# Two-layer decoder trunk: q and k halves of a pair run together, values a pair later, weight gaps behind first blocks, last gate pieces in two PSUM banks

## The chip, the cores and the metric

One Trainium2 chip, one core of it. The metric is device time in microseconds of one launch of the whole kernel; smaller is better. The time before is the median of three runs, and one further execution was profiled.

## The reference

Two pre-norm residual layers on a sequence of 256 tokens with width 1024, all in float32. Layer 0 mixes tokens with forgetting attention (a cumulative log gate is added to the causal logits), layer 1 with block attention, whose one block of 256 holds the whole sequence, so that it is causal attention with a T5 relative bias. Each layer is followed by a SwiGLU of width 2816 and a gated per-layer input.

```python
for i in range(DEPTH):                                  # DEPTH = 2
    u = _rmsnorm(h, attn_norm_g[i])
    proj = u @ w_in                                     # 1024 -> q, k, v (layer 0: and 16 forget logits)
    o = attention(q, k, v)                              # 16 heads of 64, causal, softmax in float32
    h = h + _merge_heads(o) @ w_o
    u = _rmsnorm(h, ffn_norm_g[i])
    gu = u @ ffn_w_in[i]                                # 1024 -> 2 x 2816
    h = h + (jax.nn.silu(gu[..., :D_FF]) * gu[..., D_FF:]) @ ffn_w_out[i]
    gate = jax.nn.sigmoid(_rmsnorm(h, ple_norm_g[i]) @ ple_w_gate[i])
    h = h + gate * (p[i] @ ple_w_up[i])
return _rmsnorm(h, final_norm_g)
```

## The kernel before, in words

**Numbers.** A float32 product is made of three passes in the faster type fp32r: each operand is split into a rounded part `hi` and a rest `lo`, and `mm3` issues hi*hi, hi*lo and lo*hi (lines 82, 83 and 84). Transposes (`tp`, `pp`), a part of the scores (`sp<-qkt`, line 409), of the values (`po<-tf,vf`, line 458) and a few small products (`pb`, `pr`) run in plain float32.

**Weights.** They come from DRAM in 216 halves of 128 x 1024 floats, in the order of use. `half` (lines 122 to 139) issues the load of one on SyncE's queue into `raw` (six buffers), ScalarE writes its rounded copy to `whi`, VectorE the rest to `wlo` (six buffers each, used as rings). Eight blocks of 128 x 128 lie in a half that is used as stationary operand. `APART = 16` sets where the first of them begins in its buffer, in elements of four bytes. A half that `blocks(entry)` loads with entry on has its first two blocks of `wlo` 8 elements further (`FURTHER`) and the other six 64 further (`LINE`); `whi` stays as it was.

**Attention.** First the values for all heads (`v`, four PSUM banks), then eight pairs of heads. For pair j, `project(j, 0)` makes q and `project(j, 1)` k: 8 blocks of 3 matmuls of 256 columns each, 24 per half, into one bank `pq`; behind the second VectorE and ScalarE scale and split them (`qkt`, `qkh`, `qkl`). `scores(j)` multiplies q and k of both heads on 64 rows of the array (`sp`; in layer 0 the gate is added by a further matmul), and VectorE and ScalarE make the softmax into `e`. `transposes(j)` turns the probabilities (`pp`, evacuated as `th`, `tl`, `tf`), `values(j)` multiplies them with the values (`po`). These steps are staggered, in an order written out by hand (lines 461 to 471):

```python
for j in range(NP):
    project(j, 0)
    if j >= 1:
        scores(j - 1)
    if j >= 2:
        transposes(j - 2)
    project(j, 1)
    if j >= 2:
        values(j - 2)
```

Behind the loop the remaining steps of pairs 5 to 7 alternate with halves of the output projection (`wo`).

**SwiGLU.** 22 blocks of 128 columns, `gu`: 24 matmuls for the gate and 24 for the up part. Blocks 0 and 1 run interleaved by k, with the transposes `tp` of the second half of `h` in front of k = 3. Between block 2's two halves stand the small fp32 products `pr` that spread the norm. From block 4 on, two blocks (96 matmuls of 256 columns) alternate with two steps of the down projection (`fo`, 512 columns). Of block 2 the second half, and of each even block from 4 on the first half, is loaded with entry on.

**End.** The gate of layer 1 ends in four pieces of 256 columns (two groups of rows t, two column pieces i): `part(t, i)` applies the sigmoid (`pgt`, line 601), multiplies and adds on VectorE (lines 602, 603), and squares and sums for the final norm on ScalarE (`sqf`, line 635). GpSimd makes the norm's factor (`colf`, lines 670, 671), then the rows are scaled (lines 672 to 676) and written out (line 653). Both pieces of t = 1 lie in one bank. PSUM has eight banks, all of one pool. Tiles wait for their buffers by semaphores; the engines otherwise run their queues in order.

Of the kernel before, what the change touches and what calls it, by code (L numbers as in the profile page):

```python
# [27 lines left out]
F32 = mybir.dt.float32  # L28
# [4 lines left out]
P = 128  # L33
# [24 lines left out]

ENTRY = 2
FURTHER = 8  # L60


@with_exitstack
def trunk(ctx: ExitStack, tc: tile.TileContext, x, xt, pt, w, wf, cst, pick, gains, gf, bf, rel, hot, rvm, out):
# [50 lines left out]
    def half(at=0, entry=0):  # L115


        i = state["next"]
        state["next"] += 1
        raw = work.tile([P, HW], F32, tag="raw", bufs=RAW, name=f"raw{i}")  # L120
        hi = work.tile([P, HW + LINE], F32R, tag="whi", bufs=6, name=f"whi{i}")[:, at:at + HW]
        lt = work.tile([P, HW + 2 * LINE], F32R, tag="wlo", bufs=6, name=f"wlo{i}")
        lo = lt[:, at:at + HW]
        if entry:
            nc.sync.dma_start(raw, w[i])
            nc.scalar.activation(hi, raw, AF.Copy)  # L126
            ats = [(at + FURTHER, 0, entry), (at + LINE, entry, HW)]
            for a, c0, c1 in ats:
                nc.vector.tensor_tensor(lt[:, a + c0:a + c1], raw[:, c0:c1], f32(hi[:, c0:c1]), op=ALU.subtract)  # L129
            return hi, [lt[:, a + k * P:a + (k + 1) * P] for a, c0, c1 in ats for k in range(c0 // P, c1 // P)]  # L130
        parts = 2 if i < 2 else 1
        for q in range(parts):
            c = slice(q * HW // parts, (q + 1) * HW // parts)
            if i == 0 and q == 1:
                nc.sync.dma_start(hx[:, 1], xt[:, 1])
            nc.sync.dma_start(raw[:, c], w[i][:, c])
            nc.scalar.activation(hi[:, c], raw[:, c], AF.Copy)  # L137
            nc.vector.tensor_tensor(lo[:, c], raw[:, c], f32(hi[:, c]), op=ALU.subtract)  # L138
        return hi, lo

    def blocks(entry=False):

        hi, lo = half(APART, ENTRY * P if entry else 0)
        hi = [hi[:, k * P:(k + 1) * P] for k in range(KT)]
        return hi, lo if entry else [lo[:, k * P:(k + 1) * P] for k in range(KT)]

# [91 lines left out]
    for t in (f32(vhi), f32(vlo), vf):  # L238
        nc.gpsimd.memset(t[:, :, DH:2 * DH], 0.0)

    fh, fl = (one.tile([P, KT, 4, 32], F32R, name=n) for n in ("fh", "fl"))
    for t in (fh, fl):
        nc.gpsimd.memset(f32(t)[:, :, :, H:], 0.0)

    def split(hi, lo, src):
# [25 lines left out]
    def fox_bias(nm):  # L271


        split(fh[:, :, :, 0:H], fl[:, :, :, 0:H], wf32.unsqueeze(2).to_broadcast([P, KT, 4, H]))
        pf = bank("pf")
# [59 lines left out]
    def attention(layer, nm, mid, early, nf):  # L335
# [49 lines left out]
        def project(j, a):  # L385
            hi, lo = blocks()
            if a == 0:
# [107 lines left out]
    def ffn(layer, nm, filler, np_):  # L495
# [3 lines left out]
        def up(fs):  # L499
# [96 lines left out]
    def ple(layer, nm, ut, nx):  # L596

        def gate(bk, t, c0, c1):
            at = slice(c0, c1)
            sg = work.tile([P, HC], F32, tag="t2k", bufs=3, name=f"pgt{layer}_{t}_{c0}")[:, 0:c1 - c0]  # L600
            nc.scalar.activation(sg, bk[:, c0 % HC:(c1 - 1) % HC + 1], AF.Sigmoid, scale=nm.col[:, t:t + 1])
            nc.vector.tensor_tensor(sg, sg, ut[:, t, at], op=ALU.mult)
            nc.vector.tensor_tensor(h[:, t, at], h[:, t, at], sg, op=ALU.add)

        bks = [[bank(f"pg{layer}_{hf}_{t}") for t in range(2)] for hf in range(2)]
# [26 lines left out]
        def square(t, i, c0, c1):  # L632

            sq = work.tile([P, HC], F32, tag="t2k", bufs=3, name=f"sqf{t}_{i}")
            nc.scalar.activation(sq[:, 0:c1 - c0], h[:, t, c0:c1], AF.Square, scale=D ** -0.5,
                                 accum_out=ss[:, t, i:i + 1])
# [7 lines left out]
        def part(t, i):  # L644
            c0 = HC + i * S
            gate(bks[1][t], t, c0, c0 + S)
            square(t, 1 + i, c0, c0 + S)
            if i == 0:
                nc.vector.tensor_tensor(ms[:, t, 1:2], ms[:, t, 0:1], ss[:, t, 1:2], op=ALU.add)
                nc.vector.tensor_tensor(ys[:, t, HC:HC + S], h[:, t, HC:HC + S], gb[:, HC:HC + S], op=ALU.mult)  # L650

        def rows(t, c0, c1, queue):
            queue.dma_start(out[t * P:(t + 1) * P, c0:c1], ys[:, t, c0:c1])

        for t in range(2):
            if t == 0:
                for c in range(4):
                    pair_unit(bks[1], c, wts[c], nm.k, (t,))
                part(t, 0)
            else:  # L660
                for i in range(2):
                    for k in range(KT):
                        c0 = (k % 2) * HC + i * S
                        tokens(bks[1][t][:, i * S:(i + 1) * S], nm.k(k), t, [w[:, c0:c0 + S] for w in wts[k // 2]],
                               k == 0, k == KT - 1)
                    if i == 0:
                        part(t, 0)
            part(t, 1)
            r = col[:, t:t + 1]
            nc.gpsimd.tensor_tensor(r, ss[:, t, 2:3], ms[:, t, 1:2], op=ALU.add)  # L670
            nc.gpsimd.tensor_tensor(r, r, nhalf[:, 0:1], op=ALU.pow)
            nc.scalar.activation(ys[:, t, 0:HC], ys[:, t, 0:HC], AF.Copy, scale=r)
            rows(t, 0, HC, nc.scalar)
            nc.vector.scalar_tensor_tensor(ys[:, t, HC + S:D], h[:, t, HC + S:D], r, gb[:, HC + S:D],
                                           op0=ALU.mult, op1=ALU.mult)
            nc.vector.tensor_scalar(ys[:, t, HC:HC + S], ys[:, t, HC:HC + S], r, None, op0=ALU.mult)
            rows(t, HC, D, nc.sync)

    for layer in range(2):
# [8 lines left out]
        nm = Norm(3) if layer == 0 else None  # L688
        ple(layer, np_, got[0], nm)


# [93 lines left out]
```

## Time and profile before

| | us |
|---|---|
| median of 3 runs | 674.04 (673.87 to 674.23) |
| the profiled execution | 674.86 |
| its span, first to last instruction | 673.0 |
| TensorE busy in the span | 661.4 |
| VectorE busy | 453.2 |
| ScalarE busy | 385.8 |

The profile is of one execution. In a row of the timeline stand the start and the duration in us, the engine (PE is TensorE's matmul, PEld its weight load, DVE VectorE, ACT ScalarE, POOL GpSimd, SP SyncE), the line, the operation, and output<-inputs with shape and count; in brackets, idle time of the engine before it and what ended it. Matmuls are pipelined: each lasts longer than the distance to the next, so that the distance between starts is what one costs. A row of the stages gives a window, its length, then each engine's busy time and count, the granted clock, the share of the DMA engines and GB/s. A row of the waits gives who waited for whom: total us, times, longest. The granted clock over the span was 0.997.

### The profile page before, as it was taken

Reading aid. Unit: us, or ns where it says so; the run is one execution under the profiler, and the core shown is the slowest. Engines: PE = TensorE matmul, PEld = TensorE weight load, DVE = VectorE, ACT = ScalarE, POOL = GpSimd, SP = SyncE. Lnnn points to the kernel's source line nnn. Section 1 sums busy time; section 2 is a strip of 40 time slices with the busy share of each in tenths; the row PEclk is TensorE's granted clock in tenths of the full one; section 3 lists DMA queues with packets and bytes.
Section 4 is the critical chain, followed back from the end, with each engine's and each line's share of the span. In section 5 each row is a group of like instructions: output and inputs, shape, how many; then the busy total and the mean of one; then the engine's idle time right before and its main releaser. Section 6 shows DMA issues by size and latency. Waiting matters only on the chain.

```text
span 673.0 us, 11820 instructions
## 1 busy us (share of the span) xinstructions
PE 661.4 (98%) x4620; PEld 607.0 (90%) x4620; DVE 453.2 (67%) x804; ACT 385.8 (57%) x697; POOL 10.0 (1%) x26
## 2 busy tenths in 40 slices
PE   8999999999999999999999999999999999999994
PEld 6889998999999999998889999889999999999884
DVE  5688775676666666666676888765766666666673
ACT  6876675564444444547666766655544444454663
POOL 2000000000000000000000000000000000000000
PEclk9999999999999999999999999999999999999998
DMA  8976334456555556555585533353755555565401
GB/s 277 384 279 237 126 127 129 153 170 207 193 196 195 199 188 208 193 197 174 185 286 199 172 127 126 107 175 107 241 195 193 197 197 188 188 212 195 173 1 62
DMA packets 37063, 123.78 MB, mean 184 GB/s; under 512 B 4288, under 2 KB 7056, under 8 KB 37008
## 3 DMA queue, kind: packets, MB, share of 16 engines
q1 hardware_dynamic: 36128, 121.35, 53.3%
q10 hardware_dynamic: 848, 1.68, 0.7%
q8 instruction: 36, 0.59, 0.3%
q14 instruction: 19, 0.16, 0.1%
q0 software_dynamic: 32, 0.01, 0.0%
HBM read 121.94 MB, written 4.22 MB: 187 GB/s over the span
## 4 chain that ended last, share of the span: by engine, by line
PE 92%; DMA 3%; ACT 2%; DVE 1%; issue 1%; SPq 0%; POOLq 0%; DVEq 0%; POOL 0%; ACTq 0%
PE gu L83 12%; PE gu L82 12%; PE gu L84 12%; PE fo L83 6%; PE fo L82 6%; PE fo L84 6%; PE pq L82 4%; PE pq L84 4%; PE pq L83 4%; DMA raw<-w 2%; PE wo L82 2%; PE wo L84 2%; PE wo L83 2%; PE pg L82 2%; PE pg L84 2%; PE pg L83 2%
## 5 line engine op out<-in xcount | busy, mean ns | idle before, releaser
L138 DVE TENSOR_TENSOR wlo<-raw,whi 128x1024 fp32r<-128x1024 f32 (+1 forms) x198 | 239.7, 1214 | 141.1 <-ACT whi L137 140.9
L137 ACT ACTIVATE whi<-raw 128x1024 fp32r<-128x1024 f32 (+1 forms) x198 | 207.2, 1050 | 159.3 <-PE gu L83 46.7
L82 PE MATMUL gu<-g,whi 128*128 128x256 f32 x704 | 195.5, 278 | 0.0
L84 PE MATMUL gu<-g,wlo 128*128 128x256 f32 x704 | 195.1, 277 | 0.0
L83 PE MATMUL gu<-g,whi 128*128 128x256 f32 x704 | 195.1, 277 | 0.0
L82 PEld LDWEIGHTS gu<-g,whi 128*128 128x128 f32 x704 | 132.6, 188 | 0.8
L83 PEld LDWEIGHTS gu<-g,whi 128*128 128x128 f32 x704 | 132.3, 188 | 0.7
L84 PEld LDWEIGHTS gu<-g,wlo 128*128 128x128 f32 x704 | 132.2, 188 | 0.0
L82 PE MATMUL pq<-g,whi 128*128 128x256 f32 x256 | 73.9, 289 | 0.0
L84 PE MATMUL pq<-g,wlo 128*128 128x256 f32 x256 | 71.8, 280 | 0.0
L83 PE MATMUL pq<-g,whi 128*128 128x256 f32 x256 | 71.7, 280 | 0.0
L82 PE MATMUL fo<-whi,fh 128*128 128x512 f32 x176 | 68.9, 391 | 0.0
L83 PE MATMUL fo<-wlo,fh 128*128 128x512 f32 x176 | 68.7, 390 | 0.0
L84 PE MATMUL fo<-whi,fl 128*128 128x512 f32 x176 | 68.5, 389 | 0.0
L82 PEld LDWEIGHTS pq<-g,whi 128*128 128x128 f32 x256 | 48.1, 188 | 1.0 <-ACT vhi L373 0.6
L84 PEld LDWEIGHTS pq<-g,wlo 128*128 128x128 f32 x256 | 48.7, 190 | 0.0
L83 PEld LDWEIGHTS pq<-g,whi 128*128 128x128 f32 x256 | 48.4, 189 | 0.0
L246 ACT ACTIVATE fh<-sg 128x256 fp32r<-128x256 f32 x44 | 18.2, 418 | 48.5 <-DVE sg L533 48.5
L129 DVE TENSOR_TENSOR wlo<-raw,whi 128x256 fp32r<-128x256 f32 (+1 forms) x40 | 26.0, 688 | 22.8 <-ACT whi L126 22.8
L84 PEld LDWEIGHTS fo<-whi,fl 128*128 128x128 f32 x176 | 33.1, 188 | 7.1
L82 PEld LDWEIGHTS fo<-whi,fh 128*128 128x128 f32 x176 | 33.1, 188 | 6.3
L83 PEld LDWEIGHTS fo<-wlo,fh 128*128 128x128 f32 x176 | 33.1, 188 | 6.0
(146 smaller groups left out, 967.1 us busy)
## 6 DMA issues: line engine op xcount, KB each, us to landing
raw<-w SPq DMA_DIRECT2D x214, 512.0 KB, 3.3
d<-d SPq DMA_DIRECT2D x4, 768.0 KB, 7.8
bias<-d SPq DMA_DIRECT2D x4, 512.0 KB, 5.2
raw<-w SPq DMA_DIRECT2D x4, 256.0 KB, 5.2
h<-x ACTq DMA_DIRECT2D x2, 512.0 KB, 5.3
hx<-xt SPq DMA_DIRECT2D x3, 256.0 KB, 5.1
p<-pt SPq DMA_DIRECT2D x2, 256.0 KB, 3.5
end<-gf SPq DMA_DIRECT2D x1, 512.0 KB, 4.4
```

The costliest lines, as they stand in the source:

```text
L82: mm(o, ah, bh, start=start, stop=False, skip_group_check=True)
L83: mm(o, ah, bl, start=False, stop=False, skip_group_check=True)
L84: mm(o, al, bh, start=False, stop=stop, skip_group_check=True)
L129: nc.vector.tensor_tensor(lt[:, a + c0:a + c1], raw[:, c0:c1], f32(hi[:, c0:c1]), op=ALU.subtract)
L137: nc.scalar.activation(hi[:, c], raw[:, c], AF.Copy)
L138: nc.vector.tensor_tensor(lo[:, c], raw[:, c], f32(hi[:, c]), op=ALU.subtract)
L246: nc.scalar.activation(hi, src, AF.Copy)
```

## The change

1. **Order in attention.** A pair's two projections stand together; then values three pairs back, scores one pair back, transposes two pairs back. Behind the loop the order is written anew.
2. **Gaps.** A new loader `gapped` reads halves that lie in DRAM with 56 zero columns behind their first block (1080 columns; every row of the weight array in DRAM is now that long, and other halves read the first 1024). In `whi` and `wlo` alike the block used first begins 8 elements further than before and the other seven 64 further. It is used for the first half of pairs 2 to 7, for one half of SwiGLU block 0 (there with block 3, the first behind the transposes, moved to the front), and for the second half of block 2, which had entry on before.
3. **Buffers.** `raw` is 1088 columns wide, `whi` 1152; `fh` and `fl`, the split weights of the forget gate, lie in one place of the `whi` and `wlo` rings instead of tiles of their own.
4. **End.** The second column piece of t = 1 has a bank of its own (`pgl`). The first rows' scaling is put behind the last gate and the last square on ScalarE, as two pieces; their output is one DMA on SyncE's queue. The final norm's weights are multiplied in ahead for the last column piece too. The last four weight halves begin at element 48 (`AHEAD`) instead of 0.

```diff
-ENTRY = 2
 FURTHER = 8
+ENTRY = (0, 1)
+GAP = LINE - FURTHER
+WW = HW + GAP
+AHEAD = 48
...
+    def gapped(first=0):
+        i = state["next"]
+        state["next"] += 1
+        raw = work.tile([P, HW + LINE], F32, tag="raw", bufs=RAW, name=f"raw{i}")
+        at = slice(APART + FURTHER, APART + FURTHER + WW)
+        ht, lt = (work.tile([P, HW + 2 * LINE], F32R, tag=n, bufs=6, name=f"{n}{i}")[:, at] for n in ("whi", "wlo"))
+        nc.sync.dma_start(raw[:, 0:WW], w[i])
+        nc.scalar.activation(ht, raw[:, 0:WW], AF.Copy)
+        nc.vector.tensor_tensor(lt, raw[:, 0:WW], f32(ht), op=ALU.subtract)
+        cs = [bool(n) * GAP + n * P for n in (_entered(first).index(k) for k in range(KT))]
+        return [[t[:, c:c + P] for c in cs] for t in (ht, lt)]
...
         def project(j, a):
-            hi, lo = blocks()
+            hi, lo = gapped() if j > 1 and a == 0 else blocks()
...
         for j in range(NP):
             project(j, 0)
+            project(j, 1)
+            if j >= 3:
+                values(j - 3)
             if j >= 1:
                 scores(j - 1)
             if j >= 2:
                 transposes(j - 2)
-            project(j, 1)
-            if j >= 2:
-                values(j - 2)
...
+        wo(0, 0)
+        values(NP - 3)
+        scores(NP - 1)
+        wo(1, 0)
         transposes(NP - 2)
-        wo(0, 0)
-        scores(NP - 1)
+        wo(0, 1)
         values(NP - 2)
-        wo(1, 0)
-        wo(0, 1)
         transposes(NP - 1)
         wo(1, 1)
         wo(0, 2)
...
-                wts = {f: (blocks(), blocks()) for f in fs}
+                wts = {f: (blocks() if f else gapped(3), blocks()) for f in fs}
...
-                wt = blocks(a == 1 if fs[0] == 2 else a == 0 and fs[0] % 2 == 0)
+                if fs[0] == 2 and a:
+                    wt = gapped()
+                else:
+                    wt = blocks(ENTRY if fs[0] % 2 == 0 and a == 0 and fs[0] > 2 else ())
...
-        wts = [half() for _ in range(4)]
+        wts = [half(AHEAD) for _ in range(4)]
...
+        for c in range(4):
+            pair_unit(bks[1], c, wts[c], nm.k, (0,))
+        for i in range(2):
+            part(0, i, bks[1][0])
+        lb = (bks[1][1], bank("pgl"))
+        for i in range(2):
+            for k in range(KT):
+                c0 = (k % 2) * HC + i * S
+                tokens(lb[i][:, i * S:(i + 1) * S], nm.k(k), 1, [w[:, c0:c0 + S] for w in wts[k // 2]],
+                       k == 0, k == KT - 1)
+            last = part(1, i, lb[i])
+
+        for ins, c in zip(last, (slice(0, HC), slice(HC, D))):
+            with tc.issue_after(ins.ins):
+                nc.scalar.activation(ys[:, 0, c], ys[:, 0, c], AF.Copy, scale=col[:, 0:1])
+        rows(0, 0, D, nc.sync)
+        nc.scalar.activation(ys[:, 1, 0:HC], ys[:, 1, 0:HC], AF.Copy, scale=col[:, 1:2])
+        rows(1, 0, HC, nc.scalar)
+        nc.vector.tensor_scalar(ys[:, 1, HC:D], ys[:, 1, HC:D], col[:, 1:2], None, op0=ALU.mult)
+        rows(1, HC, D, nc.sync)
```

More of the change, by code (lines that the diff above doesn't have):

```diff
@@ L119, in half @@
         state["next"] += 1
[L120 to L123, printed above, removed]
+        raw = work.tile([P, HW + LINE], F32, tag="raw", bufs=RAW, name=f"raw{i}")
+        ht, lt = (work.tile([P, HW + 2 * LINE], F32R, tag=n, bufs=6, name=f"{n}{i}") for n in ("whi", "wlo"))
+        hi, lo = ht[:, at:at + HW], lt[:, at:at + HW]
         if entry:
-            nc.sync.dma_start(raw, w[i])
-            nc.scalar.activation(hi, raw, AF.Copy)
+            nc.sync.dma_start(raw[:, 0:HW], w[i][:, 0:HW])
+            nc.scalar.activation(hi, raw[:, 0:HW], AF.Copy)
             ats = [(at + FURTHER, 0, entry), (at + LINE, entry, HW)]
@@ L139, in half, with blocks @@
         return hi, lo
[L141 to L145, printed above, removed]
+    def blocks(entry=()):
+        hi, lo = half(APART, len(entry) * P)
+        return [[t[k] if isinstance(t, list) else t[:, k * P:(k + 1) * P] for k in range(KT)] for t in (hi, lo)]
+    def gapped(first=0):
+        i = state["next"]
+        state["next"] += 1
+        raw = work.tile([P, HW + LINE], F32, tag="raw", bufs=RAW, name=f"raw{i}")
+        at = slice(APART + FURTHER, APART + FURTHER + WW)
[5 more added lines that the diff above has]
+        return [[t[:, c:c + P] for c in cs] for t in (ht, lt)]
     class Norm:
@@ L271, in fox_bias @@
     def fox_bias(nm):
+        fh, fl = (work.tile([P, HW + 2 * LINE], F32R, tag=t, bufs=6, name=n)[:, 0:HW].rearrange(
+            "p (k r c) -> p k r c", k=KT, r=4) for n, t in (("fh", "whi"), ("fl", "wlo")))
+        for t in (fh, fl):
+            nc.gpsimd.memset(f32(t)[:, :, :, H:], 0.0)
         split(fh[:, :, :, 0:H], fl[:, :, :, 0:H], wf32.unsqueeze(2).to_broadcast([P, KT, 4, H]))
@@ L652, in rows @@
         def rows(t, c0, c1, queue):
             queue.dma_start(out[t * P:(t + 1) * P, c0:c1], ys[:, t, c0:c1])
[L655 to L677, printed above, removed]
@@ L689, in trunk, with _entered, _gapped @@
         ple(layer, np_, got[0], nm)
+def _entered(first):
+    return [first] + [k for k in range(KT) if k != first]
+def _gapped(a, first=0):
+    t = a.reshape(P, KT, P)[:, _entered(first)].reshape(P, HW)
+    return np.concatenate([t[:, :P], np.zeros((P, GAP), t.dtype), t[:, P:]], axis=1)
 def _rows(a):
@@ L739 @@
         seq += _rows(wi[:, 2 * D:3 * D])
[L740 removed]
+        seq += [_gapped(a) if n > 3 and n % 2 == 0 else a for n, a in enumerate(_cols(wi[:, :D], wi[:, D:2 * D]))]
         seq += [_wide(wo, 2 * c, hf) for hf, c in ((0, 0), (1, 0), (0, 1), (1, 1), (0, 2), (1, 2), (0, 3), (1, 3))]
         a = _cols(fin[i][:, :DFF], fin[i][:, DFF:])
+        a[0], a[5] = _gapped(a[0], 3), _gapped(a[5])
         o = _rows(fout[i])
```

27 lines of the change are left out of this document (14 added, 13 removed).

## The prediction

> **What bounds it now.** I read the page's first part, then the chain of waits, then TensorE's timeline, looking for the spacing of the matmuls' starts.
>
> ```profile
> span 673.0 us, 11820 instructions
> PE 661.4 (98%) x4620; PEld 607.0 (90%) x4620; DVE 453.2 (67%) x804; ACT 385.8 (57%) x697; POOL 10.0 (1%) x26
> PE 92%; DMA 3%; ACT 2%; DVE 1%; issue 1%; SPq 0%; POOLq 0%; DVEq 0%; POOL 0%; ACTq 0%
> ```
>
> TensorE has work queued nearly all the time and is 92% of the chain that ended last. So a change pays only if it shortens TensorE's own stream, removes one of its few stalls, or shortens the tail behind it. The stream does not run at one speed:
>
> ```profile
> 37.24 0.28 PE L84 MATMUL pq<-g,wlo 128*128 128x256 f32 x1
> 39.96 0.28 PE L84 MATMUL pq<-g,wlo 128*128 128x256 f32 x1
> 69.81 0.28 PE L83 MATMUL pq<-g,whi 128*128 128x256 f32 x1
> 72.40 0.28 PE L84 MATMUL pq<-g,wlo 128*128 128x256 f32 x1
> 145.23 0.28 PE L82 MATMUL gu<-g,whi 128*128 128x256 f32 x1
> 148.05 0.28 PE L82 MATMUL gu<-g,whi 128*128 128x256 f32 x1
> 159.10 0.28 PE L82 MATMUL gu<-g,whi 128*128 128x256 f32 x1
> 161.82 0.28 PE L82 MATMUL gu<-g,whi 128*128 128x256 f32 x1
> ```
>
> These are first and last rows of four unbroken stretches of the same shape. Pair 0's projections: 24 steps in 2.72 us, 113.3 ns each. A later pair: 22 steps in 2.59 us, 117.7 ns. SwiGLU block 3: 24 steps in 2.82 us, 117.5 ns. Block 4: 24 in 2.72 us, 113.3 ns. I call these the quick and the slow pitch, 4.3 ns apart. In the timeline a stretch keeps its pitch until something breaks the stream. Slow are: pair 1's second half and pairs 2 to 7 of both layers, and blocks 0 to 3 of both layers. All blocks from 4 on are quick, and those are the ones whose even member enters from `fo` with two blocks of `wlo` shifted by 8 elements.
>
> **Pitch in attention.** Pairs 0 and 1 now run as one stretch of 96 matmuls, so pair 1's second half (24) stays quick without any gap. Pairs 2 to 7 (6 x 48 = 288 matmuls) each enter behind an fp32 transpose or the scores, with block 0 of both `whi` and `wlo` 8 elements further. If that tips them to the quick pitch, a layer gains 312 x 4.3 = 1.34 us, and the six fp32r matmuls of `po` behind pairs 3 to 7 inherit it: 30 x 4.3 = 0.13. Tipping itself costs something:
>
> ```profile
> 156.35 0.28 PE L82 MATMUL gu<-g,whi 128*128 128x256 f32 x1
> 142.31 0.36 PE L82 MATMUL gu<-g,whi 128*128 128x256 f32 x1
> ```
>
> Block 4's first 24 take 159.10 - 156.35 = 2.75 us, 0.03 more than quick; six entries, 0.18. Net 1.3 us a layer, 2.6 in both. Against it: the half that starts at 142.31, behind the fp32 matmuls of `pr`, carries the same old shift of `wlo` and leads into the slow stretch at 145.23. So a shift of 8 is no guarantee behind fp32; the new form differs by shifting the `whi` block too.
>
> The Trainium skill ("TensorE: Matmul & The Clock Gate", Part 2, "What happens when you issue a matmul") gives TensorE two independent read ports, one for the moving operand and one for the weights; and "SBUF — State Buffer" (Specifications) 16-byte lines, on which a start 32 bytes further is as well aligned as before. By these the place of a block changes nothing. The two pitches of one shape above say that something besides shape counts, but not that this shift controls it; so it is a rival below.
>
> **Pitch in the SwiGLU.** Blocks 0 and 1 behind the transposes `tp` (k = 3 to 7, 60 matmuls), block 2's first half (24), then behind `pr` block 2's second half and block 3 (72): 156 x 4.3 = 0.67 us, less two entries of 0.03, so 0.6 a layer, 1.2 in both.
>
> **Regrouping.** Per pair the order was half, scores, transposes, half, values; it becomes half, half, values, scores, transposes.
>
> ```profile
> 67.81 0.28 PE L84 MATMUL pq<-g,wlo 128*128 128x256 f32 x1
> 68.02 0.49 PE L409 MATMUL sp<-qkt 64*128 64x128 f32 x4
> 68.26 0.37 PE L412 MATMUL sp<-qkh 64*128 64x256 f32 x2
> 68.46 0.29 PE L412 MATMUL sp<-qkl,qkh 64*128 64x256 f32 x2
> 68.98 0.87 PE L443 MATMUL pp<-ident,e 128*128 128x128 f32 x6
> 69.61 0.36 PE L82 MATMUL pq<-g,whi 128*128 128x256 f32 x1
> 72.52 0.28 PE L82 MATMUL po<-th,vhi 128*128 128x256 f32 x1
> 73.23 0.61 PE L458 MATMUL po<-tf,vf 128*128 128x128 f32 x4
> 73.59 0.36 PE L82 MATMUL pq<-g,whi 128*128 128x256 f32 x1
> ```
>
> Going from 128 rows to the scores' 64 the last projection takes 68.02 - 67.81 = 0.21 us instead of 0.12: 0.09 us. That switch is not removed: scores still come eight times a layer, now mostly behind `po`. Entering `po` costs nothing (72.40 to 72.52 is one slow pitch). Of two returns from fp32 to the projections a pair, one goes. A return takes 0.20 us for its first projection (69.61 to 69.81), 0.08 over the pitch, but just ahead of it the fp32 starts are packed closer (four in 0.36 us from 73.23 to 73.59, against six in 0.63 from 68.98 to 69.61), so it is worth between 0 and 0.08 a pair, and I take the low end: 0.05 us a layer for all regrouping. The trace has no step from fp32 on 128 rows to fp32 on 64; its bounds are no cost (the 10 of both layers' loops then gain 0.9 us more) and twice 0.09 (0.9 us less). I take 0.09, the nearest row.
>
> A stall does go:
>
> ```profile
> 42.89 0.49 PE L409 MATMUL sp<-qkt 64*128 64x128 f32 x4
> 44.41 0.39 PE L412 MATMUL sp<-qkl,qkh 64*128 64x256 f32 x2 [0.69 <-DVE qkl L247]
> 45.02 0.39 PE L82 MATMUL pq<-g,whi 128*128 128x256 f32 x1
> PEld po L458 <- ACT tf L448: 0.2, 1, 0.2
> ```
>
> The first scores of layer 0 took 45.02 - 42.89 = 2.13 us against 0.96 (68.02 to 68.98), waiting for VectorE's `qkl`. Now 24 more projections (2.72 us) stand ahead of them, over twice the excess, so 1.2 us goes. The 0.2 us wait of layer 1's values for `tf` goes too, because they stand a pair further back. Together 1.4.
>
> What is late next? At a pair's end ScalarE and VectorE now meet `qkt`, a weight half, `qkh`/`qkl`, the output, two softmaxes and the transposes' evacuation in a row.
>
> ```profile
> L138 DVE TENSOR_TENSOR wlo<-raw,whi 128x1024 fp32r<-128x1024 f32 (+1 forms) x198 | 239.7, 1214 | 141.1 <-ACT whi L137 140.9
> 56.44:99.96 43.52, 43.52 (x389) 41.88 (x388) 34.81 (x107) 29.65 (x82) 0.00 (x0) 1.00 0.40 134
> 72.35 0.42 ACT L448 ACTIVATE tf<-pp 128x128 f32<-128x128 f32 x2
> ```
>
> In this stage VectorE is busy 34.81 of 43.52 us, 80%; the pair becomes some 3% shorter, so about 82%. Transposes to values were 72.52 - 69.61 = 2.91 us, and `tf` came at 72.77, 0.25 us after values began but before their fp32 part. In the loop the distance becomes a whole pair of halves, 48 x 0.1133 = 5.4 us, and the values lie a step later as well: cover of over 2 us. Only behind the loop (`values(5)` one `wo` half behind `transposes(5)`, `values(6)` likewise) is it as short as before with the longer queue ahead: 0.1 us a layer lost, bounds 0 and 0.5. The gapped halves are 1080 columns instead of 1024, 5% more ScalarE, VectorE and DMA work for 8 of 54 halves a layer; DMA is busy 0.40 here and these engines are ahead of TensorE by several halves, so nothing; without that cover 5% of VectorE's 1.214 us for each of 16 halves, 1 us in all. `fh` and `fl` take one of the ring's six places early in layer 0; hidden as the ring is filled ahead, and one fill late, 1.2 us, if not.
>
> **The last pieces.**
>
> ```profile
> 658.06 0.28 PE L82 MATMUL pg<-whi,g 128*128 128x256 f32 x1
> 660.82 0.28 PE L84 MATMUL pg<-whi,g 128*128 128x256 f32 x1
> 662.50 0.39 PE L82 MATMUL pg<-whi,g 128*128 128x256 f32 x1 [1.40 <-ACT pgt L601]
> 665.36 0.28 PE L84 MATMUL pg<-whi,g 128*128 128x256 f32 x1
> 658.26 0.48 ACT L601 ACTIVATE pgt<-pg,col 128x256 f32<-128x256 f32 x1 [1.93 <-PE pg L84]
> 660.16 0.46 ACT L601 ACTIVATE pgt<-pg,col 128x256 f32<-128x256 f32 x1
> 661.99 0.46 ACT L601 ACTIVATE pgt<-pg,col 128x256 f32<-128x256 f32 x1
> 663.73 0.42 DVE L602 TENSOR_TENSOR pgt<-pgt,ut 128x256 f32<-128x256 f32 x1
> 665.67 0.47 ACT L601 ACTIVATE pgt<-pg,col 128x256 f32<-128x256 f32 x1 [0.52 <-PE pg L84]
> 668.54 0.72 ACT L672 ACTIVATE end<-end,colf 128x512 f32<-128x512 f32 x1 [0.94 <-POOL colf L671]
> 669.29 0.38 ACTq L653 DMA_DIRECT2D out<-end  x1
> ```
>
> The last 24 matmuls waited until 662.50 because they write the bank that the gate still reads. In a bank of their own they follow at once: the last starts at about 660.94 + 23 x 0.12 = 663.7, and its gate could start 0.31 later (665.36 to 665.67), at 664.0. But ScalarE is in order: gate, square, gate. The spacing of gates where nothing else held them is 660.16 - 658.26 = 1.90, so from 661.99 the last gate is free at 663.9. VectorE's multiply, now at 663.73 behind the first rows' scaling, moves up since that scaling is moved off VectorE, behind the last gate and the last square on ScalarE. So the last gate starts at 664.0, not 665.67: 1.7 us. From there to the last issue of a DMA (669.29) the chain is the same 3.6 us; the two moved scalings (0.72 each by the row at 668.54) fit into ScalarE's waits for `h` and for `colf`. The first rows' whole 512 KB now leave about 1 us before the last ones instead of 5 us; sharing the queues costs 0 to 0.4 us, and I take 0.1. Net 1.6. The shift AHEAD of 48 can speed these 48 matmuls, but ScalarE then holds the chain, so nothing.
>
> **Sum.** 2.6 + 1.2 + 0.1 + 1.4 - 0.2 + 1.6 = 6.7 us. The profiled execution took 674.86 us (span 673.0 and 1.9 around it), 0.82 above the median of 674.04. So 674.86 - 6.7 = 668.2 on that footing, 667.3 as a median.
>
> **Rivals.** (1) The gaps do not tip the stream behind fp32 work, as the half behind `pr` suggests. Then only pair 1's half remains of the pitch, 2 x 0.1, and 2.6 + 1.2 - 0.2 = 3.6 us is missing: 670.9. This is also the case that the change doesn't do what it says. Partly tipped, attention alone: 668.5; chance 0.15 for partly, 0.2 for not at all. For it: no entry behind fp32 with a shift is quick in this trace. Against: pair 0 (quick at 37.24) enters behind the fp32 matmuls of `pb`, so fp32 ahead does not forbid it. (2) Slower: bunched evacuations become a wait. Place: `values(j-3)` and the scores' banks wait for ScalarE and VectorE at every pair. VectorE's 20% idle must then not be usable in the new order. It decides when the wait exceeds 6.7 / 16 = 0.42 us a pair over 16 pairs; at 0.6 us it gives 677. The 1.07 us by which `qkl` was late once shows that such waits exist; the 2 us of cover speak against. Chance 0.04. (3) Rival 1 with about half of such a wait, which cancels: within 0.2%, chance 0.04.
>
> **Numbers.** My forecast has 0.57; 0.2% is 1.35 us, about what a measurement of this kernel can tell from no change. Faster: 0.57 + 0.15 + 0.2 = 0.92; same 0.04; slower 0.04. The range reaches down by the free switch (0.9) and the other bounds to 665.8, and up to include rival 1 at 671.0.
>
> **What would show it.** After: projections of pairs 2 to 7 at 113 ns, blocks 2 and 3 likewise; no wait of `sp` for `qkl`; no wait of `pg` for `pgt`; last gate 1.9 us behind the one before. Wrong if those stretches stay at 117.7, or TensorE shows waits at `po` or `sp`.

## The result and the profile after

| | us |
|---|---|
| before, median of 4 runs beside the changed kernel | 674.13 (673.87 to 674.28) |
| after, median of 4 runs | 669.68 (669.48 to 669.80) |
| ratio, 95% interval | 0.9933 (0.9917 to 0.9949) |
| profiled execution, before and after | 674.86 and 669.8 |

The change makes the kernel 4.45 us faster by the medians and 5.0 us by the spans of the two profiles; forecast were 667.3 and a range of 665.8 to 671.0. One later profiled execution, of a repeat of the changed kernel, was disturbed as a whole (2345.92 us) and no stage of it is used.

The page after has these lines on the bound:

```profile
span 668.0 us, 11833 instructions
PE 656.7 (98%) x4620; PEld 603.0 (90%) x4620; DVE 455.2 (68%) x801; ACT 385.7 (58%) x698; POOL 10.3 (2%) x26
PE 97%; DMA 1%; ACT 1%; DVE 1%; SPq 0%; issue 0%; POOLq 0%; POOL 0%; ACTq 0%
```

TensorE still has 98% of the span, with the same 4620 matmuls in 4.7 us less. So the stream itself got shorter. The pitch is most easily read in the view of one tile, which gives the durations of a line's matmuls (minimum, median, maximum in ns) and the first and last start. Where the starts stand 113.3 ns apart a row has 276 ns as its median, at 117.7 ns it has 281. After, layer 0's pairs 0, 2 and 3, layer 1's pairs 2, 3 and 4, and the head of the first SwiGLU:

```profile
L88 PE MATMUL pq<-g,whi x16: 276/276/283, 35.5 to 40.6; 128*128 128x256 f32 x16
L88 PE MATMUL pq<-g,whi x16: 277/281/283, 47.5 to 52.8; 128*128 128x256 f32 x16
L88 PE MATMUL pq<-g,whi x16: 276/276/279, 55.0 to 60.1; 128*128 128x256 f32 x16
L88 PE MATMUL pq<-g,whi x16: 281/281/283, 372.1 to 377.4; 128*128 128x256 f32 x16
L88 PE MATMUL pq<-g,whi x16: 281/281/281, 379.3 to 384.6; 128*128 128x256 f32 x16
L88 PE MATMUL pq<-g,whi x16: 276/276/284, 387.7 to 392.8; 128*128 128x256 f32 x16
L88 PE MATMUL gu<-g,whi x52: 276/276/284, 130.6 to 148.5; 128*128 128x256 f32 x52
```

Pair 2 of both layers and pair 3 of layer 1 stayed slow, with the gap. The rest of the forecast quick stretches are quick.

**By stages.** This table holds, for every kernel of this document with a usable profile, the start of pair 0's first projection (`start`) and the lengths of the stages behind it. Each is the difference between the starts of two first matmuls (of `pq`, `gu`, `fo`, layer 1's `pq` and so on, and `pg` of layer 1), the last the difference to the span, which is given to 0.1 us. `head` is SwiGLU blocks 0 to 3; `rest` is from the first `fo` to layer 1's `pq`, and from there to `pg` in layer 1.

| kernel | start | attention 0 | head 0 | rest 0 | attention 1 | head 1 | rest 1 | tail |
|---|---|---|---|---|---|---|---|---|
| before | 34.51 | 92.43 | 23.94 | 211.29 | 90.05 | 23.94 | 164.66 | 32.18 |
| after | 35.28 | 90.24 | 23.18 | 211.29 | 89.15 | 23.18 | 164.69 | 30.99 |
| e1_rows | 35.01 | 90.24 | 23.17 | 211.29 | 89.16 | 23.17 | 164.70 | 30.96 |
| e2_nogaps | 35.44 | 90.22 | 23.51 | 211.26 | 89.92 | 23.56 | 164.69 | 31.00 |
| e3_oldtail | 34.65 | 90.24 | 23.17 | 211.29 | 89.16 | 23.17 | 164.70 | 32.12 |
| e4_before_rows | 35.10 | 91.33 | 23.94 | 211.29 | 90.04 | 23.94 | 164.66 | 32.20 |
| e5_pair2 | 36.65 | 90.26 | 23.18 | 211.28 | 88.76 | 23.18 | 164.69 | 31.00 |
| e6_order | 35.52 | 91.41 | 23.32 | 211.29 | 89.79 | 23.32 | 164.66 | 30.99 |
| e7_rows_split | 33.61 | 90.24 | 23.51 | 211.26 | 89.15 | 23.51 | 164.66 | 30.46 |
| e8_ahead0 | 35.38 | 90.25 | 23.17 | 211.29 | 89.16 | 23.17 | 164.70 | 31.08 |
| e9_rows_again | 33.80 | 90.24 | 23.52 | 211.25 | 89.15 | 23.52 | 164.65 | 30.47 |
| best_a | 35.40 | 90.29 | 23.18 | 211.28 | 88.76 | 23.18 | 164.69 | 30.02 |
| best_b | 36.05 | 90.26 | 23.51 | 211.25 | 88.76 | 23.51 | 164.66 | 30.10 |

Two things stand out. Behind the start, a stage that an edit doesn't touch mostly repeats to 0.01 us, so that a profile can measure an edit's worth far more sharply than the times do. Not always: attention 0 of before and e4, the heads of e7 and e9 and the tails of best_a and best_b moved by 0.3 to 1.1 us without an edit to them, and are taken up below. The start varies by 3 us, and with it the times. After minus before: +0.77 start, -2.19, -0.76, 0, -0.90, -0.76, +0.03, -1.19 tail: -5.0 us.

### The profile page after: what moved, and what is told of

The parts are those of the page before. It is cut to its first block, busy times and chain, and to the rows that moved or that the text cites. A ratio compares the mean times of both kernels' runs of the same rounds, so it can differ in the third digit from the quotient of the medians.

```text
span 668.0 us, 11833 instructions
## 1 busy us (share of the span) xinstructions
PE 656.7 (98%) x4620; PEld 603.0 (90%) x4620; DVE 455.2 (68%) x801; ACT 385.7 (58%) x698; POOL 10.3 (2%) x26
## 4 chain that ended last, share of the span: by engine, by line
PE 97%; DMA 1%; ACT 1%; DVE 1%; SPq 0%; issue 0%; POOLq 0%; POOL 0%; ACTq 0%
PE gu L89 12%; PE gu L88 12%; PE gu L87 12%; PE fo L87 6%; PE fo L88 6%; PE fo L89 6%; PE pq L87 4%; PE pq L88 4%; PE pq L89 4%; PE v L87 2%; PE wo L87 2%; PE v L89 2%; PE v L88 2%; PE wo L89 2%; PE wo L88 2%; PE pg L89 2%
## 5 line engine op out<-in xcount | busy, mean ns | idle before, releaser
L142 DVE TENSOR_TENSOR wlo<-raw,whi 128x1024 fp32r<-128x1024 f32 (+1 forms) x184 | 222.5, 1213 | 122.7 <-ACT whi L141 112.8
L141 ACT ACTIVATE whi<-raw 128x1024 fp32r<-128x1024 f32 (+1 forms) x184 | 192.2, 1049 | 152.3 <-PE gu L88 46.9
L87 PE MATMUL pq<-g,whi 128*128 128x256 f32 x256 | 72.2, 282 | 0.0
L88 PE MATMUL pq<-g,whi 128*128 128x256 f32 x256 | 71.0, 277 | 0.0
L133 DVE TENSOR_TENSOR wlo<-raw,whi 128x256 fp32r<-128x256 f32 (+1 forms) x36 | 23.4, 689 | 22.7 <-ACT whi L130 22.7
```

The costliest lines, as they stand in the source:

```text
L87: mm(o, ah, bh, start=start, stop=False, skip_group_check=True)
L88: mm(o, ah, bl, start=False, stop=False, skip_group_check=True)
```

## The experiments

The kernel before was timed on the same chip beside each group of runs: 674.74 us beside e1 to e4, 674.35 beside e5 to e8, 674.39 beside the repeat and the two best, 674.51 beside e9. Ratios are to these.

**Longer rows in DRAM** (e1_rows and e4_before_rows), from both sides:

```diff
 # e1: changed kernel; gapped halves from an array wg of their own
-        nc.sync.dma_start(raw[:, 0:WW], w[i])
+        nc.sync.dma_start(raw[:, 0:WW], wg[i])
 # e4: kernel before; w's rows padded to 1080 columns
-            nc.sync.dma_start(raw, w[i])
+            nc.sync.dma_start(raw, w[i][:, 0:HW])
```

> The changed kernel, but the 16 gapped halves come from a DRAM array of their own (1080 wide), and all other halves again from an array 1024 wide, so that their rows lie end to end. Of the 5.0 us between the two profiled spans, the start up to the first projection of pair 0 speaks against the change: 34.51 us before, 35.28 after. Theory A: rows of 4320 bytes instead of 4096 make the first loads land later (7.59 instead of 7.02 us), so the first projection starts at about 34.5 here and the time falls by 0.5 to 0.8 us, to about 669.0. Rival B: the start differs from one execution to another, whatever the rows: the first projection stays within 0.2 of 35.28 or varies, and the time stays within 0.2 us of 669.7.

> The kernel before with only its weight array's rows lengthened from 1024 to 1080 columns (the added 56 are not loaded). It asks the question of the start from the other side. Theory A (the longer DRAM rows delay the first loads): first projection of pair 0 at about 35.3 instead of 34.51 us, and 0.5 to 0.8 us more than before. Rival B (it varies by execution, or something else in the change moves it): no change within 0.2 us.

e1 took 668.69 us, ratio 0.9912 (0.9899 to 0.9926), its start 35.01 us; e4 674.49, ratio 0.9998 (0.9990 to 1.0007), its start 35.10. In e4 nothing is lost: rival B. e1's time is lower than the changed kernel's, but its stages behind the start are the same, so any gain must lie in the start; and starts vary by themselves. The rows of the stages view for 6.5 to 12 us (window, length, busy times of PE, PEld, DVE, ACT and POOL, granted clock, DMA share, GB/s) show one reason; in this order before, after, e5 and e7:

```profile
6.50:12.00 5.50, 5.21 (x16) 4.02 (x17) 4.43 (x9) 4.83 (x10) 0.38 (x1) 1.00 1.02 397
```

```profile
6.50:12.00 5.50, 4.53 (x12) 3.33 (x13) 4.16 (x9) 4.31 (x9) 0.80 (x2) 0.69 1.04 401
```

```profile
6.50:12.00 5.50, 4.70 (x11) 3.32 (x12) 4.04 (x9) 4.16 (x9) 0.84 (x2) 0.56 1.04 407
```

```profile
6.50:12.00 5.50, 4.86 (x20) 3.73 (x21) 4.55 (x9) 4.71 (x10) 0.78 (x2) 1.00 1.04 401
```

In 5.5 us 11 to 20 matmuls ran. A cold one (at half the granted clock) of 512 columns stands 427 ns from the next, a warm one 227. Over the profiles 0 to 14 of the first `v` matmuls ran cold; the profile with none (e7) has its pair 0 at 33.61 us, the one with 14 (e5) at 36.65. The clock of 1.00 in the row of before misleads: its record begins only at 10.16 us, and 7 of that profile's `v` matmuls ran cold. The Trainium skill ("TensorE: Matmul & The Clock Gate", Part 1, "What's actually happening") says that the gate watches a free-running window, so that one kernel shows 6, 11 or 14 cold matmuls by where its start falls; the 0 to 14 here are of that kind, over a wider range.

The other reason is a wait of the first `v` matmuls for `whi`, the rounded weights: none in before, 0.7 us in after, 0.2 in e1, 0.5 in e4 and up to 0.9 in e2. Before and after both begin `v` at 6.79 us and have about as many cold matmuls (7 and 6), so the later start of after is mostly this wait. Whether e1's rows shorten it is left open.

**The scores' wait.** e4 shows more. Its first scores against those of the kernel before in the prediction:

```profile
43.48 0.49 PE L409 MATMUL sp<-qkt 64*128 64x128 f32 x4
43.92 0.28 PE L412 MATMUL sp<-qkl,qkh 64*128 64x256 f32 x2
44.42 0.39 PE L82 MATMUL pq<-g,whi 128*128 128x256 f32 x1
```

They take 44.42 - 43.48 = 0.94 us, without any wait: the same instructions, with TensorE 0.59 us later and VectorE's `qkl` 0.68 us earlier (begun at 42.99 instead of 43.67). But its second scores wait for `qkl`:

```profile
50.07 0.49 PE L409 MATMUL sp<-qkt 64*128 64x128 f32 x4
50.94 0.39 PE L412 MATMUL sp<-qkl,qkh 64*128 64x256 f32 x2 [0.26 <-DVE qkl L247]
51.55 0.33 PE L443 MATMUL pp<-ident,e 128*128 128x128 f32 x1
```

They take 1.48 us where the profile before has 0.96. e6 below, in the order of before too, has the same 0.5 us at the same place, and none of the ten profiles in the new order has such a wait. So a wait for `qkl` belongs to the order of before; its place and its 1.2 us belonged to one execution, and in the two others it was 0.5.

Between these two scores stand 48 projections, with the same instructions at the same places in SBUF. In e4 they are quick, in before slow (e4, then before):

```profile
L83 PE MATMUL pq<-g,whi x16: 276/276/280, 44.6 to 49.8; 128*128 128x256 f32 x16
L83 PE MATMUL pq<-g,whi x16: 278/281/281, 45.2 to 50.5; 128*128 128x256 f32 x16
```

With the two halves that follow, this makes 0.4 us. So of the 2.19 us that attention 0 is shorter after than before, 1.1 is there in e4 as well, without the new order and without gaps.

**Without the gaps** (e2_nogaps):

```diff
-            hi, lo = gapped() if j > 1 and a == 0 else blocks()
+            hi, lo = blocks()
...
-                wts = {f: (blocks() if f else gapped(3), blocks()) for f in fs}
+                wts = {f: (blocks(), blocks()) for f in fs}
```

> The changed kernel without the gaps: first halves of pairs 2 to 7, the first half of SwiGLU block 0 and the second half of block 2 are laid out as before; order, tail and DRAM rows as changed. Theory: the gap sets the pitch of the stretch behind it. Then the projections of layer 0's pairs 3 to 7 and layer 1's pairs 4 to 7 return from 113 to 117.7 ns (9 x 48 x 4.4 ns = 1.9 us, and 0.2 us in the values behind them) and SwiGLU blocks 0 to 3 lose 0.76 us a layer: 3.6 us in all, about 673.3. Rival: the new order alone makes the attention quick (pairs enter behind scores or transposes that now end differently) and the gaps matter in the SwiGLU only: 1.5 us, about 671.2. Second rival: the gaps do nothing: 669.7.

671.38 us, ratio 0.9953 (0.9940 to 0.9965). The stages say 1.5 us: nothing in layer 0, 0.77 in layer 1, 0.33 and 0.38 in the heads. Layer 0's pairs 2, 3 and 4, layer 1's pair 4 and the first head up to `pr`:

```profile
L88 PE MATMUL pq<-g,whi x16: 276/276/280, 47.7 to 52.8; 128*128 128x256 f32 x16
L88 PE MATMUL pq<-g,whi x16: 281/281/281, 54.9 to 60.2; 128*128 128x256 f32 x16
L88 PE MATMUL pq<-g,whi x16: 276/276/283, 63.5 to 68.6; 128*128 128x256 f32 x16
L88 PE MATMUL pq<-g,whi x16: 281/281/281, 388.1 to 393.4; 128*128 128x256 f32 x16
L88 PE MATMUL gu<-g,whi x28: 281/281/281, 130.8 to 140.3; 128*128 128x256 f32 x28
```

The first rival has the right total (671.2) and the right share for layer 0, but not for layer 1, and the heads lose half of what it took. Pairs 3 and 4 of layer 0 have the same layout and both enter behind transposes, one slow and one quick. So a layout doesn't decide by itself.

**The order of before, with the gaps** (e6_order; behind the loop likewise):

```diff
             project(j, 0)
-            project(j, 1)
-            if j >= 3:
-                values(j - 3)
             if j >= 1:
                 scores(j - 1)
             if j >= 2:
                 transposes(j - 2)
+            project(j, 1)
+            if j >= 2:
+                values(j - 2)
```

> The changed kernel with the order of before in the attention, in the loop and behind it: half, scores, transposes, half, values two pairs back. Gaps, SwiGLU and tail as changed. Attention stages were 92.43 and 90.04 before, 90.24 and 89.16 after; without the gaps 90.23 and 89.92. Theory O (the order carries nearly all of layer 0's 2.2 us): 1.2 us of waiting for the keys' residue comes back, and of the pitch only the gapped first halves behind the values can be quick, 6 x 24 x 4.4 ns = 0.6 us: 91.8 and 89.4, so the time is 1.8 us above the changed kernel, or 3.1 if those halves stay slow. Rival L (the layout carries the pitch, the order only the stall): 91.5 and 89.2, 1.3 us above.

672.11 us, ratio 0.9967 (0.9955 to 0.9980). Attention comes to 91.41 and 89.79 us, the heads to 23.32 each; by stages this is 2.1 us above the changed kernel, between theory O and its worse branch. A row of layer 1 that holds pieces of two pairs:

```profile
L88 PE MATMUL pq<-g,whi x19: 281/281/281, 386.8 to 395.9; 128*128 128x256 f32 x19
```

Both halves of a pair are slow there, gap or not. For the four combinations the waits in the order of before are left out: 0.5 us for `qkl` in e4 and e6 (second scores of layer 0), and in e4's layer 1 the 0.2 us for `tf` that the prediction found in before and that e6 doesn't have. What is left, for layer 0 and layer 1:

| | order before | order after |
|---|---|---|
| no gaps | 90.8, 89.8 (e4) | 90.22, 89.92 (e2) |
| gaps | 90.9, 89.79 (e6) | 90.24, 89.15 (after) |

In layer 0 the order brings 0.6 to 0.7 us, with gaps or without, and gaps add nothing to it. In layer 1 neither gains anything alone, and both together bring about 0.7. One difference remains in the upper row: e4 has the buffers of before and e2 the new ones (point 3 of the change), which no run undid alone. In the lower row only the order differs.

**Other layouts for pair 2** (e5_pair2):

```diff
-            hi, lo = gapped() if j > 1 and a == 0 else blocks()
+            hi, lo = gapped() if j > 2 and a == 0 else blocks(ENTRY if layer and j == 2 and a == 0 else ())
```

> The changed kernel with another layout for one half a layer: the first half of pair 2 has no gap in layer 0 (as in the kernel without gaps, where layer 0's pair 2 ran at 113.3 ns while it runs at 117.7 with the gap), and in layer 1 only the residue's first two blocks stand 8 elements further. Read in the attention stages, 90.24 and 89.16 us in the changed kernel. Theory H (what sets the pitch is the history of the stream as much as the layout): layer 0's pair 2 is quick, 0.21 us gained, and pair 3, which was slow behind a quick pair 2 without a gap, may be slow or quick with it: 90.03 if quick, 90.24 if slow; layer 1's pair 2 stays slow or tips, with pair 3 behind it: 89.16 or down to 88.7. Rival G (a gap of both blocks is what tips a stream behind fp32 matmuls, and what the exceptions show is the scores ahead of them): layer 0's pair 2 is slow as with the gap, 90.24, and layer 1 is unchanged.

One run, 670.81 us with a late start; attention 90.26 and 88.76. Layer 0's pairs 2 and 3, layer 1's pairs 2 and 3:

```profile
L88 PE MATMUL pq<-g,whi x16: 276/276/280, 48.9 to 54.0; 128*128 128x256 f32 x16
L88 PE MATMUL pq<-g,whi x16: 281/281/281, 56.1 to 61.4; 128*128 128x256 f32 x16
L88 PE MATMUL pq<-g,whi x16: 276/276/284, 373.4 to 378.6; 128*128 128x256 f32 x16
L88 PE MATMUL pq<-g,whi x16: 276/276/284, 380.5 to 385.6; 128*128 128x256 f32 x16
```

Layer 0's pair 3, with its gap untouched, was quick behind a slow pair 2 (after) and is slow behind a quick one. Layer 1's pair 3 goes the other way. This is theory H: what ran before counts as much as the layout. In layer 1 it is worth 0.39 us.

**The tail of before** (e3_oldtail):

```diff
-        wts = [half(AHEAD) for _ in range(4)]
+        wts = [half() for _ in range(4)]
...
-        lb = (bks[1][1], bank("pgl"))
...
-                tokens(lb[i][:, i * S:(i + 1) * S], nm.k(k), 1, [w[:, c0:c0 + S] for w in wts[k // 2]],
+                        tokens(bks[1][t][:, i * S:(i + 1) * S], nm.k(k), t, [w[:, c0:c0 + S] for w in wts[k // 2]],
```

> The changed kernel with the tail of before: the last tile's two pieces in one bank, no shift of its weights by 48, scalings in their old places. Theory: the tail is worth what the two profiles show from the first gate matmul to the end, 1.2 us: about 670.9, with the 24 matmuls of 512 columns of the first tile at 226.7 ns again instead of 233.5 (0.16 us back) and the last 48 at 120 instead of 113.3. Rival: the chain of gates on its own is worth 1.7 us, and the end of the changed kernel is late by 0.5 us for another reason that varies from one execution to another: about 671.4 and a wider spread of the changed kernel's times.

671.00 us, ratio 0.9950 (0.9937 to 0.9964); its tail is 32.12 us against 30.99, 1.13 us. The theory's size held. The rival's late end is not excluded by it: best_a below ends 0.4 us sooner with the same last gates.

**Where 0.4 us of the tail stayed.** The gates and the last issues of the changed kernel's DMAs, and the view of DMA issues of before and after (count, size, median us to landing):

```profile
658.31 0.46 ACT L621 ACTIVATE pgt<-pg,col 128x256 f32<-128x256 f32 x1
660.13 0.46 ACT L621 ACTIVATE pgt<-pgl,col 128x256 f32<-128x256 f32 x1
662.68 1.16 SPq L678 DMA_DIRECT2D out<-end  x2
663.73 0.37 ACTq L678 DMA_DIRECT2D out<-end  x1
```

```profile
out<-end ACTq DMA_DIRECT2D x2, 256.0 KB, 2.7
```

```profile
out<-end SPq DMA_DIRECT2D x1, 512.0 KB, 2.6
out<-end ACTq DMA_DIRECT2D x1, 256.0 KB, 2.9
```

The last gate comes 1.82 us behind the one before, and the last issue 3.60 us behind the gate (3.62 before). But from that issue to the end it is 668.0 - 663.73 = 4.3 us, against 673.0 - 669.29 = 3.7. Landing explains 0.2 (2.7 and 2.9). So the first rows were sent in two pieces, each when it is ready (e7_rows_split, and the same kernel once more as e9_rows_again):

```diff
             with tc.issue_after(ins.ins):
                 nc.scalar.activation(ys[:, 0, c], ys[:, 0, c], AF.Copy, scale=col[:, 0:1])
-        rows(0, 0, D, nc.sync)
+            rows(0, c.start, c.stop, nc.sync)
```

> The changed kernel, but the first tile's rows leave in two transfers of 256 KB, each issued as soon as its half is scaled, instead of one of 512 KB. In the changed kernel's profile the last issue comes 3.60 us behind the last gate, as before (3.62), but from that issue to the end it is 4.26 us instead of 3.76: the landing is later by 0.13, and the rest, 0.37, comes behind the landing. Theory S (the late 512 KB is in the way of the last rows and of the end): landing 0.1 sooner and the end 0.4 sooner, 3.8 us from the last issue to the end. Rival E (the 0.37 belongs to the program's end whatever leaves before): 4.2 us again.

> Once more the kernel with the first tile's rows in two transfers. Its instructions, operands and places are those of the changed kernel up to the last scalings, yet its first profile had 23.51 us for the head of the SwiGLU in both layers where the changed kernel had 23.18. Theory X (the pitch of the stretch behind the transposes falls out by the execution, from a few ns of what came before): the head is 23.18 or 23.51 here, and may differ from the first profile. Rival P (the program decides, through something in it that I don't see): 23.51 in both layers again, and attention 90.24 and 89.15. For the tail both say what the first profile showed: about 4.2 minus 0.45 us from the last issue to the end, 30.49 us from the first gate matmul; in time 0.5 us below the changed kernel, about 0.9933 less 0.0007 of the kernel before.

668.24 us in one run, then 669.62, ratio 0.9922 (0.9901 to 0.9942). The tail is 30.46 and 30.47 us, 0.5 less:

```profile
662.66 0.37 ACTq L678 DMA_DIRECT2D out<-end  x1
```

```profile
out<-end SPq DMA_DIRECT2D x3, 256.0 KB, 2.0
out<-end ACTq DMA_DIRECT2D x1, 256.0 KB, 2.4
```

From the last issue to the end it is now 666.4 - 662.66 = 3.7 us. Theory S has the sum right and its parts wrong: the last rows land 0.5 us sooner (2.4 for 2.9), and what comes behind the landing stays about 1.3 us (1.4 in after), against 1.0 before. What holds it there the profile doesn't show; its cause is open.

e9 also asked why e7's heads took 23.51 us where the changed kernel's took 23.18, though up to the last scalings the instructions, operands and places are the same. It answered rival P: 23.5 in both layers again, slow on the same stretch in both (e7, then e9):

```profile
L88 PE MATMUL gu<-g,whi x28: 281/281/281, 128.9 to 138.5; 128*128 128x256 f32 x28
```

```profile
L88 PE MATMUL gu<-g,whi x28: 281/281/281, 129.1 to 138.7; 128*128 128x256 f32 x28
```

Behind pair 0 one program thus repeated its pitch, although its starts differ (33.61 and 33.80). Two programs with equal instructions there did not agree. By which property the program decides is not settled.

**AHEAD set to 0** (e8_ahead0):

```diff
-AHEAD = 48
+AHEAD = 0
```

> The changed kernel with the last four weight halves back on their old place (the shift of 48 set to 0). With the shift the 24 matmuls of 512 columns took 233.5 ns instead of 226.7, the last 48 of 256 columns 113.3 instead of 120. Theory A: the first gate comes 0.16 us sooner and the last matmul 0.16 us later; as ScalarE's row of gates holds the end, the end moves by -0.16 to +0.1 us. Rival T: the shift is what lets the last gate come 1.82 us behind the one before; without it the last gate waits for TensorE and the end is 0.3 us later.

669.99 us in one run, tail 31.08 us against 30.99. Theory A: the first gate comes sooner, the last one later, and the shift of 48 is worth 0.1 us. The last gate does wait for TensorE, as rival T had it, but 0.16 us only.

**The repeat and two sums** (r_after unchanged; best_a and best_b are e7's tail with other forms for pairs 2 and 3; best_b in full):

```diff
-            hi, lo = gapped() if j > 1 and a == 0 else blocks()
+            hi, lo = gapped() if j > 3 - layer and a == 0 else blocks(ENTRY if j == 3 - layer and a == 0 else ())
...
+            rows(0, c.start, c.stop, nc.sync)
```

> The changed kernel itself once more, beside its variants. Theory: behind the first projection of pair 0 one program runs alike in every execution, so the stages come out as in its first profile (attention 90.24 and 89.16, SwiGLU heads 23.18, tail 30.98 us), and its times differ only by the start, where the number of the first matmuls at a cold pitch of 427 ns was 1 to 14 in the profiles so far: about 669.7, 668.5 to 671. Rival: the pitch falls out differently in each execution, and a head of 23.51 or another attention stage shows up here.

> The changed kernel with what helped: the first tile's rows in two transfers (tail 30.49 instead of 30.98 us), and in both layers the first half of pair 2 without the gap, with only the residue's first two blocks 8 elements further (layer 1's attention 88.76 instead of 89.16). Layer 0's pair 2 has not been seen with this layout. If it tips and pair 3 with it: 90.03 instead of 90.24, 1.1 us below the changed kernel. If pair 2 tips and pair 3 doesn't: 0.9 below. If the layout matters less than a few ns of history: SwiGLU heads may fall to 23.51, and only 0.3 to 0.6 is left.

> As the variant before, but in layer 0 pair 2 has no shift at all (quick twice so far, 5.65 instead of 5.86 us) and pair 3 has the residue's first two blocks 8 further in place of the gap (behind a quick pair 2 the gap left it slow). If pair 3 tips: layer 0's attention 90.03, 1.1 us below the changed kernel. If it stays slow: 90.26, 0.9 below.

The repeat took 670.41 us, ratio 0.9940 (0.9926 to 0.9953), and gave no stages. best_a took 668.84, 0.9921 (0.9909 to 0.9934); best_b 668.76, 0.9909 (0.9894 to 0.9924). Both beat the kernel before; best_b's interval also lies below that of the repeat beside it, best_a's overlaps it. By stages best_a is worth 1.3 us against the changed kernel (0.39 in layer 1, 0.97 in the tail, nothing in layer 0, where pair 2 became quick with this layout and pair 3 slow) and best_b 0.6, since its heads fell to 23.51. 0.4 of best_a's tail has come on top of e7's with the same code, behind the landing: from its last issue at 663.50 to the end it is 3.3 us, not 3.7. best_a's 1.57 us against the repeat agrees with its stages; best_b's 1.65 is more than its stages give; the rest may be its starts, of which only one is on record. I would keep best_a.

## Why the prediction was right, and where it missed

Faster was right, and the range held the time. The forecast was 2.4 us too low. Of this, 1.7 us are stages and 0.7 the footing; by the prediction's steps, predicted and found:

| step | predicted | found |
|---|---|---|
| start | 0 | -0.77 |
| attention 0 | 1.3 + 0.05 + 1.2 - 0.1 = 2.45 | 2.19 |
| attention 1 | 1.3 + 0.05 + 0.2 - 0.1 = 1.45 | 0.90 |
| both heads | 1.2 | 1.52 |
| tail | 1.6 | 1.19 |
| rest | 0 | -0.03 |
| sum | 6.7 | 5.0 |

- **Pitch in attention.** The size was near, the reason half wrong, so part of the near sum is luck. The prediction gave the 2.6 us to the gaps and 0.1 to the regrouping. Without the waits layer 0 gained 1.0 us and layer 1 0.7. e2 and e6 show that the gaps have no part in layer 0's (the order brings 0.6, and 0.4 is the pitch that e4 shows without the change), and that layer 1 takes both. The step that failed is "if that tips them" for all of pairs 2 to 7: pair 2 (both layers) and pair 3 (layer 1) stayed at 117.7, 48 x 4.4 = 0.2 us each, 0.6 of the 0.8 that is missing in both layers. For the other 0.2 there is one candidate, the wait for `tf` behind the loop, listed under rival 2: 0.23 us of the weight loads in each layer, where 0.1 was taken. Rival 1 was wrong for layer 1, and right that a gap is no guarantee behind fp32 work. The two rules of the Trainium skill weighed in the prediction ("TensorE: Matmul & The Clock Gate", Part 2, and "SBUF — State Buffer", Specifications), by which a block's place changes nothing, don't account for this: with the order after, layer 1's gaps move 0.77 us without one instruction more on TensorE.
- **Regrouping.** The step that had no row, from fp32 on 128 rows to the scores' 64, came out as taken: the last `po` in front of scores stands 0.205 us from them, in front of transposes 0.111, so 0.09 more.
- **The heads.** 0.76 each instead of 0.6. Also blocks 0 and 1 ahead of the transposes run quick now (36 x 4.4 ns = 0.16), which the sum left out. e2 keeps this without any gap, keeps block 2's second half and block 3 quick too, and loses the 0.33 and 0.38 behind the transposes. That loss isn't shown to be the gap's: with the gap the same stretch is quick in seven profiles and slow in three (e7, e9, best_b).
- **The stall.** The length of the first scores fell by 1.19 us as forecast (2.13 to 0.94):

```profile
46.38 0.49 PE L425 MATMUL sp<-qkt 64*128 64x128 f32 x4
46.83 0.28 PE L428 MATMUL sp<-qkl,qkh 64*128 64x256 f32 x2
47.32 0.38 PE L87 MATMUL pq<-g,whi 128*128 128x256 f32 x1
```

  But e4 and e6, in the order of before, have only 0.5 us of such a wait. The rest belonged to the profiled execution, which stood 0.8 us above the median. Subtracting a full 1.2 us for the stall and then the 0.82 for the footing probably took part of the same thing twice; the footing came out as 0.1 us (669.8 against 669.68), and 0.7 of the miss is this.
- **The start.** +0.77 us, which no step had. It is mostly the wait for `whi`, in the third line under rival 2; the cold matmuls were about as many. e4's times show no cost of the new rows of DRAM. By the other profiles the start could as well have been -0.9.
- **The tail.** The gate's 1.7 us came (663.73 - 660.13 and 669.29 - 665.67 are alike, the gates 1.82 apart). Mis-sized was the way from the last issue to the end: 0.1 taken for the sharing of queues, 0 to 0.4 allowed; 0.5 to 0.6 measured, of which e7 got 0.5 back. Only 0.1 to 0.2 of it is a later landing; the rest comes behind the landing, and its cause is open. AHEAD, taken as nothing, is worth 0.1.
- **Rival 2**, a new wait from bunched evacuations at every pair, did not come. TensorE's matmuls waited for nothing behind the start; all that their view lists is the first three lines. The weight loads' view adds the fourth, at `values(6)` behind the loop of both layers:

```profile
PE v L87 <- ACT g L175: 1.9, 1, 1.9
PE cold L106 <- PEq L811: 0.8, 1, 0.8
PE v L87 <- ACT whi L141: 0.7, 1, 0.7
PEld po L474 <- ACT tf L464: 0.5, 2, 0.2
```

## What to carry to other kernels

Ask of a stall in a profile whether a second execution has it, and at what size, before you count it as a gain, above all close to the start and where the profiled time stands above the median. Where times scatter, compare stages between the first matmuls of two steps: most repeated to 0.01 us and priced edits of 0.1 us that the times couldn't. Take a second profile of each side even so, as attention 0 moved by 1.1 us between before and e4. When two edits meet in one stage, as order and layout here, undo each alone: their worth was not additive, and the more plausible one was not the one that paid in layer 0.

## What was not expected of the hardware

One fp32r matmul of 256 columns has two pitches, 113.3 and 117.7 ns, and a stretch mostly keeps the one it falls into. Nothing that was tried decides alone which: same layout and unlike pitch (e2's pairs 3 and 4), one pair with its layout untouched turned by its predecessor (e5), equal instructions and places quick in e4 and slow in before, where the scores ahead had waited, equal instructions unlike in two programs (after, e7), one program alike twice (e7, e9). What selects it is open. And the last 256 KB landed in 2.9 us where the first rows left in one DMA of 512 KB 1.05 us ahead, and in 2.4 where they left in two of 256 KB, 2.5 and 1.04 us ahead; size and time changed together there.
